# Differential attention and mLSTM block on one core: products of the last attention chunks some steps later, gate products in four groups of 32 output partitions

## The chip, the core and the metric

The kernel runs on one core of a Trainium2 chip. The core has engines that run side by side, each with its own queue of instructions that it works off in order: PE (TensorE, matrix products into the PSUM memory, with its weight loads, PEld), DVE (VectorE), ACT (ScalarE), POOL (GpSimd) and SP (SyncE, which here only issues transfers). Transfers (DMA) run on 16 shared DMA engines. An instruction waits at the head of its queue until what it reads has been written and the buffer that it writes has come free; everything behind it on that engine waits too. The metric is the time of one execution on the device, in microseconds (us); of several runs the median is given.

## The reference, cut to what matters

One layer over x of 1024 rows and 1024 columns. After an RMSNorm one projection gives all inputs of two branches.

```python
xn = _rmsnorm(h, norm_w[layer])
(da_q, da_k, da_v, da_z, ml_q, ml_k, ml_v, ml_o, ml_z, ml_i, ml_f,
 gate_a, gate_m) = [xn @ wp for wp in _split_columns(w_in[layer])]
y_a = _diff_attention(da_q, da_k, da_v, ...) * jax.nn.silu(da_z)
y_m = _mlstm(ml_q, ml_k, ml_v, ml_i, ml_f, ml_o, ...) * jax.nn.silu(ml_z)
merged = g_a * (y_a @ w_pa[layer]) + g_m * (y_m @ w_pm[layer])
h = h + merged @ w_out[layer]
```

The attention branch has 8 heads. For each head and each chunk of 128 queries, two softmaxes over the keys are taken (the keys end with the query's own chunk, so chunk i has (i+1)·128 of them), `attn = probs[0] - lam * probs[1]`, and `attn @ v` is normed over the head's 128 columns (`_rmsnorm(out, subln_w)`). The mLSTM branch has 8 heads as well; its input and forget gates, `ml_i` and `ml_f`, are only 16 of the 11,280 columns of the projection.

## The kernel before, in words

**Numbers as pairs.** Every large product runs in float16 with each operand split into a high and a low part: high·high, high·low and low·high are added in PSUM. So each step of a product is three matmuls: lines 330 to 332 for units with 512 columns, 359 to 361 for units with 256 columns, 856 to 858 for the products with v.

**Phases, units, slots.** The projection is cut into units of 256 weight columns. A phase works off its units on PE and weaves a side program into them. Phase 0 makes q, k, v and z of head 0 (units `aqk` and `avz`). Phases 1 to 7 make those of head h+1 and run `attention(h)`, for heads 0 to 6, as the side program; phase 8 makes gate columns and runs the attention of head 7; then come the mLSTM gates (`if_gates`), the mLSTM heads, and the last projections. A phase with two units has 64 slots, and a plan says at which slot each piece of the side program is issued: an entry (n, name) is due at slot n·8//7, and what is not due by the last slot is issued after it. `PLAN_A` is the plan of heads 0 to 6, `PLAN_C` that of head 7.

**The pieces of attention(h)** (names of the plan, with the chunk's number): `q` makes the scores of the first softmax (line 813 on PE, 823 on DVE, 827 on ACT); `r` makes those of the second, combines both (DVE 838) and turns the result: ACT casts it to float16 (845), DVE takes the low part (846), and SP issues a transposing transfer (848) that lays it down as PE needs it; `v` is the product with v on PE (856 to 858), whose squares ACT sums (859); `f` is the norm's factor for four chunks on POOL (863 to 865); `o` scales four chunks on DVE (871); `t` casts, splits and transposes the result (548 to 550). Chunks 0 to 3 of the product share one bank of PSUM and chunks 4 to 7 another.

**The gate products.** `if_proj` multiplies the 16 gate columns (high and low part side by side, 32 columns, tile `wifp`) with all of x, high and low part, and leaves a table of 32 rows and 1024 columns in device memory (`gif_d`). It runs at the end of phase 0's `aqk` unit, as 2 × 16 matmuls into two PSUM tiles `pmi` of 32 partitions (line 469); ACT copies each out with a scale (472), and SP stores it (473). Much later `if_gates` loads four pieces of it (input and forget gate, each with the high and the low weights, eight heads a piece) and adds them in pairs on DVE (485).

**Buffers around it.** PSUM has three banks `pp` for the units, one pair `psb` for the scores, two `pmi` and one `pvp`. A unit's bank is emptied by ACT and DVE (for `avz` by 568 and 564 on ACT, 569 and 565 on DVE). Tiles of 4 KB per partition come from a ring of 15. The weights of a unit are loaded by SP (226), squared on ACT (245), summed over partitions by a tiny matmul on PE (165), scaled by DVE (135 to 139), and split into parts on ACT (257) and DVE (259).

**What sets the order.** The plan and the weave set the order in which the code asks for instructions. The framework then places them on the engines' queues when the kernel is built, so that an edit can also change the order on an engine at places that it does not name.

Of the kernel before, what the change touches and what calls it, by code (L numbers as in the profile page):

```python
# [10 lines left out]
F32 = mybir.dt.float32  # L11
BF = mybir.dt.bfloat16
I32 = mybir.dt.int32
AF = mybir.ActivationFunctionType
ALU = mybir.AluOpType
AX = mybir.AxisListType

P = 128
S = 1024
D = 1024  # L20
NT = S // P
KC = D // P
H = 8
# [9 lines left out]
OFF_GATE = (9232, 10256)  # L33
BIG = 3.0e38
RING = 15
PLAN_A = [(0, 'q0'), (0, 'r0'), (0, 'q1'), (3, 'r1'), (4, 'q2'), (5, 'r2'), (9, 'q3'), (9, 'r3'), (9, 'q4'), (10, 'v0'), (14, 'v1'), (16, 'r4'), (17, 'q5'), (18, 'v2'), (19, 'r5'), (21, 'q6'), (24, 'r6'), (25, 'q7'), (27, 'r7'), (28, 'v3'), (29, 'v4'), (29, 'v5'), (30, 'f0'), (30, 'o0'), (33, 'v6'), (35, 'v7'), (42, 't0'), (43, 'f1'), (44, 'o1'), (55, 't1')]
PLAN_C = [(0, 'q0'), (0, 'r0'), (6, 'q1'), (7, 'r1'), (7, 'q2'), (9, 'r2'), (16, 'q3'), (19, 'r3'), (19, 'q4'), (19, 'r4'), (19, 'v0'), (22, 'v1'), (22, 'v2'), (25, 'q5'), (28, 'r5'), (29, 'q6'), (31, 'v3'), (32, 'v4'), (33, 'r6'), (37, 'q7'), (38, 'f0'), (38, 'r7'), (46, 'o0'), (52, 'v5'), (52, 'v6'), (63, 'v7'), (64, 'f1'), (67, 'o1'), (82, 't1'), (83, 't0')]
PLAN_M = [(0, '00gate'), (0, '01k0'), (2, '02k1'), (4, '03s0'), (5, '04s1'), (8, '05e0'), (9, '06p0'), (11, '07e1'), (13, '08p1'), (14, '09c0'), (19, '10g00'), (19, '11g01'), (20, '12g02'), (21, '13cp0'), (22, '14bs0'), (22, '15g10'), (25, '16g11'), (25, '17g12'), (26, '18cp1'), (30, '19bs1'), (30, '20g20'), (30, '21g21'), (31, '22cp2'), (32, '23bs2'), (33, '24ch'), (37, '25n0'), (47, '26t0'), (50, '27n1'), (55, '28t1')]
PLAN_N = [(0, '00gate'), (1, '01k0'), (1, '02k1'), (8, '03s0'), (10, '04s1'), (13, '05e0'), (13, '06p0'), (15, '07e1'), (16, '08p1'), (22, '09c0'), (25, '10g00'), (26, '11g01'), (26, '12g02'), (26, '13cp0'), (30, '14bs0'), (31, '15g10'), (36, '16g11'), (37, '17g12'), (40, '18cp1'), (42, '19bs1'), (43, '20g20'), (44, '21g21'), (53, '22cp2'), (54, '23bs2'), (59, '24ch'), (61, '25n0'), (67, '26t0'), (70, '27n1'), (71, '28t1')]
# [9 lines left out]
def block_kernel(ctx, tc, x, norm_w, w_in, lam, subln_w, rel_bias, conv_w, conv_b, b_if,  # L49
                 mh_w, b_gate, w_pa, w_pm, w_out, norm_final, onehot, out):  # L50
    nc = tc.nc
    v, s, g, te = nc.vector, nc.scalar, nc.gpsimd, nc.tensor
# [7 lines left out]
    dram = ctx.enter_context(tc.tile_pool(name="dram", bufs=1, space=bass.MemoryType.DRAM))  # L60
# [15 lines left out]
    def R(dt=F32, shape=None, p="r"):  # L76
        return ring.tile(shape or [P, S], dt, tag="t4", name=nm(p))
# [13 lines left out]
    def s_ps():  # L91
        return psb.tile([P, S], F32, tag="psb", name=nm("psb"))

    def m_ps():
        return pmi.tile([P, 512], F32, tag="pmi", name=nm("pmi"))
# [194 lines left out]
    def x_src(i, th):  # L290
        t = X[th, i // 2]
        return t[:, 0, i % 2, :], t[:, 1, i % 2, :]
# [75 lines left out]
    HS = [slice(0, 512), slice(512, 1024)]  # L368
# [77 lines left out]
    decb = ctile([P, H * NT], p="decb")  # L446
    mcols = ctile([P, 3, NT, H], p="mcols")
    wsc = ctile([P, NT, H], p="wsc")
    gif_d = dram.tile([32, S], F32, tag="gifd", name="gif_d")

    def if_proj():
        ss = sm(cols=2, p="wss")
        s.activation(junk(P), early[:, 384:512], AF.Square, accum_out=ss[:, 0:1])
        v.memset(ss[:, 1:2], 0.0)
        sb, isb = sm(p="sb"), sm(p="isb", bufs=8)
        fnorm_finish(ss, sb, isb)
        sig = sm(p="sig", bufs=8)
        v.tensor_tensor(sig, isb, isx, op=ALU.mult)
        parts = half_tile("wifp").bitcast(F16)[:, :256].rearrange("p (a b) -> p a b", a=KC)
        s.activation(parts[:, :, :16], wif, AF.Copy, scale=sb)  # L460
        v.scalar_tensor_tensor(parts[:, :, 16:], wif, sb, parts[:, :, :16], op0=ALU.mult, op1=ALU.subtract)
        for _ in range(8):
            yield
        t = R(shape=[32, S], p="gif")
        for th in range(2):
            gps = m_ps()
            for i in range(KC):
                for k in range(2):
                    te.matmul(gps[:32, :], parts[:, i, :], x_src(i, th)[k], start=(i + k == 0),
                              stop=(i + k == KC))  # L470
                yield
            s.activation(t[:, HS[th]], gps[:32, :], AF.Copy, scale=sig[:32, :])
        nc.sync.dma_start(gif_d, t)
        yield

    def if_gates():
        gi = R(shape=[H, NT, P], p="gi")
        ff = R(shape=[H, NT, P], p="ff")
        gl = [R(shape=[H, NT, P], p="gl") for _ in range(2)]
        for k, dst in ((0, gi), (1, ff), (2, gl[0]), (3, gl[1])):  # L480
            nc.sync.dma_start(dst.rearrange("h a b -> h (a b)"), gif_d[k * H:k * H + H, :])
        for _ in range(4):
            yield
        for k, dst in ((0, gi), (1, ff)):
            v.scalar_tensor_tensor(dst, dst, bif[:, k:k + 1], gl[k], op0=ALU.add, op1=ALU.add)
        yield
        fl = lambda t: t.rearrange("h a b -> h (a b)")
        af = R(shape=[H, NT, P], p="af")
        v.scalar_tensor_tensor(af, ff, -1.0, ff, op0=ALU.mult, op1=ALU.max)
        s.activation(af, af, AF.Exp, scale=-1.0)  # L490
        s.activation(af, af, AF.Ln, bias=1.0)
        yield
        lf = ff
        v.scalar_tensor_tensor(lf, ff, 0.0, af, op0=ALU.min, op1=ALU.subtract)
        yield
        m = R(shape=[H, NT, P], p="m")
        v.tensor_tensor_scan(fl(m), fl(lf), fl(gi), 0.0, op0=ALU.add, op1=ALU.max)
        yield
        b = af
        for c in range(NT):  # L500
            v.tensor_tensor_scan(b[:, c, :], ones[:H, :], lf[:, c, :], 0.0, op0=ALU.mult, op1=ALU.add)
        yield
        ng = R(shape=[H, NT, P], p="ng")
        v.tensor_tensor(ng, b, m, op=ALU.subtract)
        a = gi
        v.tensor_tensor(a, gi, b, op=ALU.subtract)
        yield
        mprev = ctile([H, NT], p="mprev")
        v.memset(mprev[:, 0:1], 0.0)
        v.tensor_copy(mprev[:, 1:NT], m[:, 0:NT - 1, P - 1])  # L510
        ngl = ctile([H, NT], p="ngl")
        v.tensor_copy(ngl, ng[:, :, P - 1])
        wi = lf
        v.tensor_tensor(wi, ng, mprev.unsqueeze(2).to_broadcast([H, NT, P]), op=ALU.add)
        s.activation(wi, wi, AF.Exp)
        yield
        ws = af
        v.tensor_tensor(ws, a, ngl.unsqueeze(2).to_broadcast([H, NT, P]), op=ALU.add)
        s.activation(ws, ws, AF.Exp)
        yield  # L520
        en = m
        s.activation(en, m, AF.Exp, scale=-1.0)
        dec = ctile([H, NT], p="dec")
        v.tensor_tensor(dec, ngl, mprev, op=ALU.add)
        s.activation(dec, dec, AF.Exp)
        s.dma_start(rows_d[0], fl(ng))
        s.dma_start(rows_d[1], fl(wi))
        s.dma_start(dec_d[0:1, :].rearrange("o (h c) -> (o h) c", c=NT), dec)
        s.dma_start(decb, dec_d[0:1, :].to_broadcast([P, H * NT]))
        yield  # L530
        cps = m_ps()
        for k, t in enumerate((a, ws, en)):
            for c in range(NT):
                o = (k * NT + c) * H
                te.transpose(cps[:, o:o + H], t[:, c, :], ident[:H, :H])
        v.tensor_copy(mcols.rearrange("p a b c -> p (a b c)"), cps[:, :3 * NT * H])
        v.tensor_scalar(wsc, mcols[:, 1], 0.25 * KSC, None, op0=ALU.mult)
        yield
# [529 lines left out]
    for units, side, steps in phases:  # L1068
# [6 lines left out]
        for u in units:  # L1075
# [6 lines left out]
            dst, post = consumers[u.kind](u.idx, u.w)  # L1082
# [62 lines left out]
    for ch in range(4):  # L1145
        w, so = wo[ch].w, [None, None]
        c = slice(ch * 256, ch * 256 + 256)
# [75 lines left out]
```

## Time and profile before

| | |
|---|---|
| median of 3 runs | 1428.03 us (1427.54 to 1428.84) |
| the profiled execution | 1430.35 us |
| its span, first to last instruction | 1428.5 us |
| around the span | 1.85 us |
| mean granted PE clock in the span | 0.994 |

| engine | busy us | share of span |
|---|---|---|
| PE | 1379.5 | 97% |
| PEld | 914.8 | 64% |
| DVE | 849.0 | 59% |
| ACT | 734.3 | 51% |
| POOL | 157.7 | 11% |

Times within the span count from its first instruction. A row of the timeline gives the start, the duration, the engine, the line of the kernel, the operation, the tiles out<-in and a count, and in brackets how long the engine had been idle before it and what ended that. Matmuls overlap, so the distance between two starts, not the duration in the row, is what one matmul costs in a stream. An issue of a transfer stands as SPq (issued by SP) or ACTq (issued by ACT); the transfer lands later. The granted clock is the share of TensorE's full clock that the chip allowed.

### The profile page before, as it was taken

How to read it: one execution, taken by the hardware profiler on the slowest of the kernel's cores; microseconds unless marked ns; L12 is line 12 of the kernel's file. 1: busy time of each engine (PE TensorE's matmuls, PEld its weight loads, DVE VectorE, ACT ScalarE, POOL GpSimd, SP SyncE). 2: the span in 40 equal slices, each digit the busy share in tenths (PEclk: the TensorE clock that was granted, in tenths of full speed). 3: DMA queues.
4: the chain of work that ended last, by engine and by line, in shares of the span. 5: the costliest groups of instructions: out<-in, count | busy, mean ns of one | idle time of the engine just before them, and what ended most of it. 6: DMA issues, size and time to landing. Idle time of an engine off the chain costs nothing.

```text
span 1428.5 us, 25046 instructions
## 1 busy us (share of the span) xinstructions
PE 1379.5 (97%) x9650; PEld 914.8 (64%) x9650; DVE 849.0 (59%) x2310; ACT 734.3 (51%) x1533; POOL 157.7 (11%) x215
## 2 busy tenths in 40 slices
PE   5989999999999999999999999999999999999997
PEld 3657575675756754444586687778769675444786
DVE  6267869678696766433436674765866564233633
ACT  7266657566575667732343444443435344644542
POOL 2001010010100001100102010120211200122004
PEclk9999999999999999999999999999999999999999
DMA  6457366473563634544221413221232135434303
GB/s 200 66 131 154 84 109 136 99 141 84 112 135 87 144 87 117 170 157 129 79 75 60 103 41 94 45 89 45 77 86 75 60 90 158 166 106 164 114 16 118
DMA packets 232585, 150.14 MB, mean 105 GB/s; under 512 B 117297, under 2 KB 209730, under 8 KB 232466
## 3 DMA queue, kind: packets, MB, share of 16 engines
q1 hardware_dynamic: 218450, 123.28, 35.1%
q10 hardware_dynamic: 14016, 25.27, 5.2%
q8 instruction: 75, 1.23, 0.4%
q14 instruction: 44, 0.36, 0.1%
HBM read 90.12 MB, written 18.55 MB: 76 GB/s over the span
## 4 chain that ended last, share of the span: by engine, by line
PE 77%; DVE 8%; DMA 5%; ACT 4%; POOL 3%; issue 2%; SPq 0%; POOLq 0%; DVEq 0%; ACTq 0%
PE pp L330 14%; PE pp L332 14%; PE pp L331 14%; PE pp L359 9%; PE pp L360 9%; PE pp L361 9%; PE psb L813 4%; DMA z<-z 3%; DVE z L823 2%; DMA qw<-rows_d 2%; ACT z L827 1%; DVE wp L259 1%; PE psb L909 1%; DVE z L838 1%; ACT z L845 1%
## 5 line engine op out<-in xcount | busy, mean ns | idle before, releaser
L359 PE MATMUL pp<-wp,X 128*128 128x256 f16 x1280 | 350.4, 274 | 0.0
L360 PE MATMUL pp<-wp,X 128*128 128x256 f16 x1280 | 350.3, 274 | 0.0
L361 PE MATMUL pp<-wp,X 128*128 128x256 f16 x1280 | 350.2, 274 | 0.0
L332 PE MATMUL pp<-X,wp 128*128 128x512 f16 x768 | 291.0, 379 | 1.0 <-DVE wp L259 1.0
L330 PE MATMUL pp<-X,wp 128*128 128x512 f16 x768 | 291.5, 380 | 0.3 <-ACT wp L257 0.3
L331 PE MATMUL pp<-X,wp 128*128 128x512 f16 x768 | 291.3, 379 | 0.0
L257 ACT ACTIVATE wp<-wt,sb 128x512 f16<-128x512 f32 x208 | 137.8, 712 | 110.9 <-DVE sb L138 76.2
L332 PEld LDWEIGHTS <-wp 128*128 128x128 f16 x1024 | 100.0, 98 | 119.3 <-DVE wp L259 1.5
L245 ACT ACTIVATE junk<-wt 128x1024 bf16<-128x1024 f32 x112 | 118.1, 1054 | 100.4 <-DMA wt<-in_w_in_dram 88.0
L330 PEld LDWEIGHTS <-wp 128*128 128x128 f16 x1024 | 100.2, 98 | 102.0 <-issue 1.7
L331 PEld LDWEIGHTS <-wp 128*128 128x128 f16 x1024 | 100.1, 98 | 97.2
L259 DVE SCALAR_TENSOR_TENSOR wp<-wt,sb,wp 128x512 f16<-128x512 f32 x208 | 149.9, 760 | 13.9 <-ACT wp L257 12.2
L359 PEld LDWEIGHTS <-X 128*128 128x128 f16 x1280 | 125.8, 98 | 16.5 <-issue 0.4
L360 PEld LDWEIGHTS <-X 128*128 128x128 f16 x1280 | 125.7, 98 | 16.2
L361 PEld LDWEIGHTS <-X 128*128 128x128 f16 x1280 | 125.7, 98 | 15.7
L827 ACT ACTIVATE z<-z,mx 128x256 f32<-128x256 f32 (+7 forms) x128 | 98.7, 771 | 47.5 <-DVE mx L826 27.1
L823 DVE CUSTOM_DVE_ANT_0 z<-psb,BB,negc 128x256 f32<-128x256 f32 (+7 forms) x128 | 104.1, 813 | 14.9 <-PE psb L813 14.8
L332 PE MATMUL pp<-Y,wp 128*128 128x512 f16 x256 | 97.0, 379 | 0.0
L331 PE MATMUL pp<-Y,wp 128*128 128x512 f16 x256 | 97.0, 379 | 0.0
L330 PE MATMUL pp<-Y,wp 128*128 128x512 f16 x256 | 97.0, 379 | 0.0
L650 DVE SCALAR_TENSOR_TENSOR acc<-up,wcol,acc 128x512 f32<-128x512 f32 x96 | 78.0, 828 | 27.0 <-POOL acc L651 24.8
L813 PE MATMUL psb<-K,Q 128*128 128x512 f16 (+3 forms) x384 | 83.3, 325 | 8.8 <-DMA K<-hl 4.5
(251 smaller groups left out, 2015.8 us busy)
## 6 DMA issues: line engine op xcount, KB each, us to landing
wt<-in_w_in_dram SPq DMA_DIRECT2D x128, 256.0 KB
wt<-in_w_in_dram SPq DMA_DIRECT2D x24, 512.0 KB
K<-hl SPq DMA_DIRECT2D x32, 256.0 KB
gate_d<-tg ACTq DMA_DIRECT2D x32, 256.0 KB
xt<-in_x_dram SPq DMA_DIRECT2D x8, 512.0 KB
Q<-hl SPq DMA_DIRECT2D x32, 128.0 KB
wt<-in_w_pa_dram SPq DMA_DIRECT2D x8, 512.0 KB
ft<-gate_d ACTq DMA_DIRECT2D x16, 256.0 KB
```

The lines of the kernel that those rows point to most:

```text
L245: s.activation(j, w.wt[k], AF.Square, accum_out=ss[:, k:k + 1])
L257: s.activation(dst[0], src, AF.Copy, scale=w.sb)
L259: v.scalar_tensor_tensor(dst[1], src, w.sb, dst[0], op0=ALU.mult, op1=ALU.subtract)
L330: te.matmul(ps, wh, xh, start=(start and i == 0), stop=False, **kw)
L331: te.matmul(ps, wh, xl, start=False, stop=False, **kw)
L332: te.matmul(ps, wl, xh, start=False, stop=(stop and i == n - 1), **kw)
L359: te.matmul(ps[:, o], xh[:, t], wh, start=i == 0, stop=False)
L360: te.matmul(ps[:, o], xh[:, t], wl, start=False, stop=False)
L361: te.matmul(ps[:, o], xl[:, t], wh, start=False, stop=i == KC - 1)
L813: te.matmul(sp[:, c:e], Q[:, p, i * P:(i + 1) * P], K[p][:, j, c:e], start=(j == 0), stop=(j == 1))
L823: v.tensor_tensor_reduce(z[:, :n], sp[:, :n], bb[:, S - n:], negc, BIG, op0=ALU.add, op1=ALU.min, accum_out=mx)
L827: s.activation(z[:, :n], z[:, :n], AF.Exp, bias=mx, scale=-1.0, accum_out=rr[:, 2 * i + p:2 * i + p + 1])
```

## The change

Three things change.

1. `PLAN_A`, for heads 0 to 6: the products with v of chunks 5, 6 and 7 are due later (29, 33, 35 become 30, 35, 40), and so are the factor, the scaling and the output step of the second half (43, 44, 55 become 47, 48, 58). The factor and scaling of the first half now stand ahead of `v5` in the list.
2. The gate products go into four groups of 32 output partitions of one PSUM tile `psb`: one group for each pair of half of x's rows and high or low part. The 32 matmuls keep their size; they are issued round the four groups, and each group sums over its own eight steps. One ACT instruction over 128 partitions copies all out, and ACT's queue, not SP's, stores it.
3. `if_gates` loads six pieces instead of four, each from two places, and adds two more sums on DVE; the products with the high and with the low part of x, which PE added before, are added there (low weights with low x are left out). The ring hands out two more tiles.

```diff
-PLAN_A = [(0, 'q0'), (0, 'r0'), (0, 'q1'), (3, 'r1'), (4, 'q2'), (5, 'r2'), (9, 'q3'), (9, 'r3'), (9, 'q4'), (10, 'v0'), (14, 'v1'), (16, 'r4'), (17, 'q5'), (18, 'v2'), (19, 'r5'), (21, 'q6'), (24, 'r6'), (25, 'q7'), (27, 'r7'), (28, 'v3'), (29, 'v4'), (29, 'v5'), (30, 'f0'), (30, 'o0'), (33, 'v6'), (35, 'v7'), (42, 't0'), (43, 'f1'), (44, 'o1'), (55, 't1')]
+PLAN_A = [(0, 'q0'), (0, 'r0'), (0, 'q1'), (3, 'r1'), (4, 'q2'), (5, 'r2'), (9, 'q3'), (9, 'r3'), (9, 'q4'), (10, 'v0'), (14, 'v1'), (16, 'r4'), (17, 'q5'), (18, 'v2'), (19, 'r5'), (21, 'q6'), (24, 'r6'), (25, 'q7'), (27, 'r7'), (28, 'v3'), (29, 'v4'), (30, 'f0'), (30, 'o0'), (30, 'v5'), (35, 'v6'), (40, 'v7'), (42, 't0'), (47, 'f1'), (48, 'o1'), (58, 't1')]
...
-    gif_d = dram.tile([32, S], F32, tag="gifd", name="gif_d")
+    gif_d = dram.tile([P, 512], F32, tag="gifd", name="gif_d")
...
-        t = R(shape=[32, S], p="gif")
-        for th in range(2):
-            gps = m_ps()
-            for i in range(KC):
+        t = R(shape=[P, 512], p="gif")
+        gps = s_ps()[:, :512]
+        for i in range(KC):
+            for th in range(2):
                 for k in range(2):
-                    te.matmul(gps[:32, :], parts[:, i, :], x_src(i, th)[k], start=(i + k == 0),
-                              stop=(i + k == KC))
-                yield
-            s.activation(t[:, HS[th]], gps[:32, :], AF.Copy, scale=sig[:32, :])
-        nc.sync.dma_start(gif_d, t)
+                    o = (th * 2 + k) * 32
+                    te.matmul(gps[o:o + 32, :], parts[:, i, :], x_src(i, th)[k], start=(i == 0), stop=(i == KC - 1))
+        yield
+        s.activation(t, gps, AF.Copy, scale=sig)
+        s.dma_start(gif_d, t)
         yield
...
-        gl = [R(shape=[H, NT, P], p="gl") for _ in range(2)]
-        for k, dst in ((0, gi), (1, ff), (2, gl[0]), (3, gl[1])):
-            nc.sync.dma_start(dst.rearrange("h a b -> h (a b)"), gif_d[k * H:k * H + H, :])
+        gl = [R(shape=[H, NT, P], p="gl") for _ in range(4)]
+
+        for k, dst in ((0, gi), (1, ff), (2, gl[0]), (3, gl[1]), (4, gl[2]), (5, gl[3])):
+            r = k * H if k < 4 else 32 + (k - 4) * H
+            nc.sync.dma_start(dst.rearrange("h (t a) b -> h t (a b)", t=2),
+                              gif_d.rearrange("(t r) c -> r t c", t=2)[r:r + H])
...
             v.scalar_tensor_tensor(dst, dst, bif[:, k:k + 1], gl[k], op0=ALU.add, op1=ALU.add)
+            v.tensor_tensor(dst, dst, gl[2 + k], op=ALU.add)
```

What stands on the engines' queues differs at three places. From the second half of the gate functions on, the changed kernel's line numbers are higher by 5 (856 becomes 861).

PE, head 0, where the product of chunk 7 with v begins (line 856; `z255` holds its transposed probabilities). The rows ahead are of the `avz` unit of head 1; the tiles X57, X72, X82 and X86 hold its contraction steps in this order, six matmuls to a tile. Before:

```order
L360 MATMUL pp278_1441<-wp231_1107,X86_306 128x256
L361 LDWEIGHTS X86_306
L361 MATMUL pp278_1441<-wp231_1107,X86_306 128x256
L856 LDWEIGHTS z255_1248
L856 MATMUL pmi268_1323<-vr153_644,z255_1248 128x128
```

And now:

```order
L360 MATMUL pp276_1416<-wp226_1083,X72_256 128x256
L361 LDWEIGHTS X72_256
L361 MATMUL pp276_1416<-wp226_1083,X72_256 128x256
L861 LDWEIGHTS z254_1246
L861 MATMUL pmi267_1321<-vr152_642,z254_1246 128x128
```

Two tiles of the unit, 12 matmuls, now stand ahead of it. In numbers of unit matmuls between the products of chunks 4, 5, 6 and 7: 5, 19 and 36 before, 6, 36 and 30 now, and 123 before, 111 now, between chunk 7 and the next head's first scores. The same holds for heads 0 to 6; the tiny matmul 165 keeps its place among the unit's.

ACT, head 0, around the cast of chunk 7 (line 845, now 850, the row with 128x1024 and two z tiles). The rows 859 (now 864) are the squares of chunks 3, 4, 5 and 6, and 245 squares the two halves of a later unit's weights. Before:

```order
L859 ACTIVATE junk_1339,ssq_922<-pmi_1323,rc_921 128x128
L859 ACTIVATE junk_1359,ssq_922<-pmi_1323,rc_921 128x128
L245 ACTIVATE junk_1371,wss_1370<-wt_958 128x1024
L845 ACTIVATE z_1264<-z_1248 128x1024
L245 ACTIVATE junk_1388,wss_1370<-wt_1124 128x1024
L548 ACTIVATE y_1550<-on_1377 128x512
L859 ACTIVATE junk_1423,ssq_922<-pmi_1323,rc_921 128x128
```

And now:

```order
L864 ACTIVATE junk_1337,ssq_920<-pmi_1321,rc_919 128x128
L245 ACTIVATE junk_1349,wss_1348<-wt_956 128x1024
L864 ACTIVATE junk_1378,ssq_920<-pmi_1321,rc_919 128x128
L245 ACTIVATE junk_1386,wss_1348<-wt_1122 128x1024
L850 ACTIVATE z_1262<-z_1246 128x1024
L553 ACTIVATE y_1548<-on_1355 128x512
L573 ACTIVATE vr_1288<-pp_1294 128x256
```

One square of weights moves ahead of chunk 5's, the other ahead of the cast.

ACT, at the end of phase 0, from the square of the second weights on (245). Before:

```order
L245 ACTIVATE junk159_681,wss157_672<-wt143_532 128x1024
L472 ACTIVATE gif147_600<-pmi148_601,sig125_443 32x512
L472 ACTIVATE gif147_600<-pmi149_619,sig125_443 32x512
L568 ACTIVATE vr153_644<-pp155_650 128x256
L257 ACTIVATE wp166_741<-wt128_458,sb161_724 128x512
L257 ACTIVATE wp167_756<-wt128_458,sb161_724 128x512
L564 ACT_TABLE_LOAD
L564 ACTIVATE tz152_643<-pp155_650,hs151_640 128x256
```

And now:

```order
L245 ACTIVATE junk158_679,wss156_670<-wt143_532 128x1024
L257 ACTIVATE wp165_739<-wt128_458,sb160_722 128x512
L257 ACTIVATE wp166_754<-wt128_458,sb160_722 128x512
L257 ACTIVATE wp167_769<-wt143_532,sb160_722 128x512
L257 ACTIVATE wp169_789<-wt143_532,sb160_722 128x512
L473 ACTIVATE gif147_600<-psb148_601,sig125_443 128x512
L573 ACTIVATE vr152_642<-pp154_648 128x256
L474 DMA gif_d_149<-gif147_600 128x512
L569 ACT_TABLE_LOAD
L569 ACTIVATE tz151_641<-pp154_648,hs150_638 128x256
```

All four weight parts now stand ahead of the copy of the gate products, and that copy empties `psb`, which the first scores of head 0 then write. On PE the first scores' second half (`r0`, two matmuls) has moved behind the 51 unit matmuls that followed it.

## The prediction

> **What bounds the kernel now.** I read the page's first part: which engine is busy.
>
> ```profile
> PE 1379.5 (97%) x9650; PEld 914.8 (64%) x9650; DVE 849.0 (59%) x2310; ACT 734.3 (51%) x1533; POOL 157.7 (11%) x215
> ```
>
> PE sets the end: the change is worth what it takes from PE's idle time or from PE's stream, and costs what it adds there. So next I read whom PE waited for, from the list of waits (engine, waiting line, releaser: us in total, times, longest).
>
> ```profile
> PE pmi L856 <- DMA z<-z: 10.7, 8, 2.9
> PE psb L813 <- DMA K<-hl: 4.5, 2, 2.6
> PE pmi L856 <- DVE BB L801: 1.3, 5, 0.3
> PE pmi L856 <- ACT junk L859: 0.8, 5, 0.2
> ```
>
> The products with v (856) lose 12.8 us: to the transposing transfer, and by 2.1 us to small waits at the start of chunks 5 and 6. The timeline of PE tells where the long ones are, one in each of heads 0 to 6 (the bracket is the idle time).
>
> ```profile
> 131.02 0.23 PE L856 MATMUL pmi<-vr,z 128*128 128x128 f16 x1 [0.84 <-DMA z<-z]
> 190.94 0.23 PE L856 MATMUL pmi<-vr,z 128*128 128x128 f16 x1 [1.97 <-DMA z<-z]
> 250.15 0.23 PE L856 MATMUL pmi<-vr,z 128*128 128x128 f16 x1 [1.35 <-DMA z<-z]
> 309.37 0.23 PE L856 MATMUL pmi<-vr,z 128*128 128x128 f16 x1 [1.74 <-DMA z<-z]
> 368.11 0.23 PE L856 MATMUL pmi<-vr,z 128*128 128x128 f16 x1 [0.81 <-DMA z<-z]
> 428.87 0.23 PE L856 MATMUL pmi<-vr,z 128*128 128x128 f16 x1 [2.87 <-DMA z<-z]
> 489.32 0.23 PE L856 MATMUL pmi<-vr,z 128*128 128x128 f16 x1 [0.88 <-DMA z<-z]
> ```
>
> All seven are the first matmul of chunk 7: its 24 matmuls follow. PE gets there before the turned probabilities have landed.
>
> **The plan: work moved ahead of the wait.** PE now does 12 more matmuls of the `avz` unit before chunk 7 (the rows above: X86 before, X72 of the next pass now). What one costs is read at the end of phase 0, where 144 of the same kind run without a gap; first and last row:
>
> ```profile
> 57.96 0.28 PE L359 MATMUL pp<-wp,X 128*128 128x256 f16 x1
> 73.58 0.27 PE L361 MATMUL pp<-wp,X 128*128 128x256 f16 x1
> ```
>
> (73.58 − 57.96) / 143 = 0.109 us from start to start, so 12 × 0.109 = 1.31 us of work goes ahead of each wait. A head can gain this much and no more, and no more than its idle time. Beside the waits of the rows stand 2.1 / 7 = 0.30 us a head in chunks 5 and 6 (one more unit matmul stands ahead of chunk 5, 17 more ahead of chunk 6, so these go too). Idle time by head: 1.14, 2.27, 1.65, 2.04, 1.11, 3.17, 1.18. Each cut at 1.31, the sum is **8.67 us**.
>
> This holds if the transfer lands when it did. What issues it, in head 0:
>
> ```profile
> 122.67 0.37 ACT L859 ACTIVATE junk<-pmi,rc 128x128 bf16<-128x128 f32 x1 [1.31 <-PE pmi L858]
> 123.16 1.06 ACT L245 ACTIVATE junk<-wt 128x1024 bf16<-128x1024 f32 x1
> 124.22 1.06 ACT L845 ACTIVATE z<-z 128x1024 f16<-128x1024 f32 x1
> 125.18 1.04 ACT L245 ACTIVATE junk<-wt 128x1024 bf16<-128x1024 f32 x1
> 125.30 1.23 DVE L846 TENSOR_TENSOR z<-z,z 128x1024 f16<-128x1024 f32 x1 [0.40 <-ACT z L845]
> 126.56 4.42 DMA z<-z
> ```
>
> The cast (845) at 124.22 releases DVE's low part, this the transfer at 126.56 (this last row is of the chain, where the transfer's piece lasts until it landed, 130.98), and PE starts at 131.02. Two squares of weights (245) now stand ahead of the cast instead of one. The first moves into the 1.31 us in which ACT waited for chunk 5: it takes 1.06 us (123.16 to 124.22) and fits. The second takes the place that the first had, and the cast starts when it did, or later by the one unit matmul that now stands ahead of chunk 5, 0.1 us. This costs nothing where a head's idle time is used up, and 0.1 us in the four heads where some is left (1, 2, 3, 5): **+0.4 us**. Bounds of the cast's delay: 0 (ACT's gap holds both), and 1.1 us (the first square does not fit, a whole square later). I take 0.1, by the 1.31 us gap.
>
> **The clock in head 5.** Windows of equal length after chunk 7's start in heads 5 and 0 (after the window's length: PE, PEld, DVE, ACT, POOL busy with counts, granted clock, DMA share, GB/s):
>
> ```profile
> 428.87:432.74 3.87, 3.87 (x33) 3.39 (x33) 0.51 (x1) 1.30 (x3) 0.69 (x2) 0.56 0.98 244
> 131.02:134.89 3.87, 3.87 (x48) 3.61 (x49) 2.54 (x4) 3.00 (x7) 1.92 (x3) 1.00 0.92 199
> ```
>
> After the wait of 2.87 us the granted clock was 0.56 and 15 matmuls fewer were done: 15 × 0.109 = 1.6 us. No other head shows it, so a wait near 2 us did not bring it on, and head 5 will be left with 3.17 − 1.31 = 1.9. Another execution need not have it; bounds are 0 and 1.6, I count half, **−0.8 us**, because one head of seven is too little to say how often it comes. The Trainium skill (page "TensorE: Matmul & The Clock Gate", section "What's actually happening") has PE fall to half clock after at least one idle window of about 3.4 us. The trace had it after 2.87 us, and the measurement decides; by the page's figure this term would be zero and the sum 0.8 us smaller.
>
> **The front: five microseconds of products, and who waits there.** The 32 gate products start at 50.95 and the unit behind them at 57.96: 7.01 us. What follows, on PE, ACT, DVE and SP:
>
> ```profile
> 50.95 7.08 PE L469 MATMUL pmi<-X,wifp 128*32 128x512 f16 x32
> 74.33 0.16 PE L165 MATMUL pmi<-s,ones 128*128 128x1 bf16 x1 [0.47 <-ACT gif L472]
> 77.05 0.27 PE L813 MATMUL psb<-K,Q 128*128 128x128 f16 x2 [2.56 <-DMA K<-hl]
> 79.29 0.37 PE L813 MATMUL psb<-K,Q 128*128 128x128 f16 x2 [1.96 <-DMA K<-hl]
> 79.45 0.42 PE L359 MATMUL pp<-wp,X 128*128 128x256 f16 x1
> 72.56 1.06 ACT L245 ACTIVATE junk<-wt 128x1024 bf16<-128x1024 f32 x1 [20.90 <-DMA wt<-in_w_in_dram]
> 73.61 1.23 ACT L472 ACTIVATE gif<-pmi,sig 32x512 f32<-32x512 f32 x2
> 74.75 0.36 ACT L568 ACTIVATE vr<-pp 128x256 f16<-128x256 f32 x1
> 75.14 1.33 ACT L257 ACTIVATE wp<-wt,sb 128x512 f16<-128x512 f32 x2
> 76.49 1.28 ACT L564 ACT_TABLE_LOAD   x1
> 77.79 0.47 ACT L564 ACTIVATE tz<-pp,hs 128x256 f32<-128x256 f32 x1
> 78.29 0.42 DVE L565 SCALAR_TENSOR_TENSOR tz<-tz,pp 128x256 f32<-128x256 f32 x1 [0.32 <-ACT tz L564]
> 69.32 0.35 SPq L585 DMA_DIRECT2D strip<-tb_d  x1
> ```
>
> The bill for PE is made here by transfers. ACT waits 20.90 us for weights that land at 72.5; SP issues `strip`, and behind it Q and K, only from 69.32; neither hears of PE. PE fills its three banks until 73.85 and then waits for ACT and for K. If the four groups run side by side, PE merely arrives some 5 us earlier at the same wait; if they run one behind the other, it arrives as before. Both give **0**. The Trainium skill (same page, section "Measured speedup vs the span model") has three column groups of 512 columns run 2.38 times as fast; an estimate by it is 7.01 / 2.38 = 2.9 us, a gain of 4.1, and no trace here shows it yet.
>
> What moves is the end of this wait, through ACT's new order. The tiny matmul 165 no longer waits for the copy (0.47 us sooner at most; I take 0.3), so the four parts (257, 1.33 / 2 = 0.64 apart) run from about 74.8 to 77.35. Then come the copy (1.23 / 2 = 0.62, to 77.95), `vr` (0.36), the table load (1.28, to 79.5), `tz` (0.47) and DVE's 0.42, which empties the first bank at 80.4. PE's first scores, which now need `psb` from the copy, start at 78.0, not 77.05; unit matmuls resume at 80.45, not 79.45: **+1.0 us**. Bounds: +0.5, if the half clock ends when it did so that the lost stretch is a slow one (the row at 79.45 runs 0.42, the one at 73.58 0.27); +2.7, by head 0's first turn, whose scores are now behind 51 matmuls:
>
> ```profile
> 83.70 14.14 SPq L848 DMA_TRANSPOSE z<-z  x3
> L856 PE MATMUL pvp<-vr,z x80: 219/219/219, 96.6 to 534.3; 128*128 128x128 f16 x80
> ```
>
> The turn's transfer was issued 4.4 us after those scores (79.29 to 83.70). They now come at about 88.9 (80.45, 24 matmuls at 0.21, 24 at 0.11, three at 0.22), so the transfer is issued at 93.3 and lands at 97.7 if it takes 4.42 us; chunk 0's product is due at 96.6 + 1.0. With a landing 1.6 us slower it waits 1.7.
>
> **The gates later.** Two loads and two sums more, the sums by the nearest row; the row behind it (of the chain) is where PE first reads the gates, in 24 small transposes.
>
> ```profile
> 558.76 1.27 DVE L485 SCALAR_TENSOR_TENSOR ff<-ff,bif,gl 8x1024 f32<-8x1024 f32 x1
> 646.67 1.58 PE pmi L535 x24
> ```
>
> 2 × 1.27 = 2.5 us on DVE, 88 us ahead of PE's first use. The cover is PE's own stream of gate and output units in between, in which the list of waits has no entry for the gates. I count **0**; without the cover 2.5. The loads stand on SP ahead of chunk 7's transfer of head 7 and wait for transfers alone.
>
> **Sum:** −8.67 + 0.4 − 0.8 + 0 + 1.0 + 0 = −8.1 us. The profiled execution took 1430.35 (span 1428.5 and 1.85 around it), 2.3 above the median of 1428.03; the terms are differences, so I take them from the median: 1428.03 − 8.1 = **1419.9 us**. Ends of this case: −8.67 − 1.6 + 0.5 = −9.8, or 1418.2; and with a cast 0.5 us late in all seven heads, no clock term and the dear front, −8.67 + 3.5 + 2.7 = −2.5, or 1425.5.
>
> **The rivals.**
>
> *The landing moves along.* If the first square does not fit into ACT's gap, the cast and the transfer come 1.06 us later, and of 1.31 us moved only 0.25 a head is left: −1.75 + 1.0 = −0.7, or 1427.3. For it: both squares do stand ahead of the cast, and the spare time is 1.31 − 1.06 = 0.25 us. Against: ACT's wait there ended with PE's chunk 5, which hardly moves. Chance 0.13.
>
> *The gate products' time reaches the end.* If four groups run as one, 7.01 × 3/4 = 5.3 us more go: 1414.6. It needs transfers that land with PE. Against it: 69.32 and 72.56 are set by transfers. The Trainium skill's rule on column groups, named above, speaks for the speed, not for the place. Chance 0.04.
>
> *Slower: the cast waits for weights.* The second square now runs at about 123.2 ahead of the cast, and its weights were needed only at 125.18. If they land as late as that, the cast comes 2.05 us later, which the 1.31 us no longer cover: 0.74 × 7 = 5.2, with the front +6.2, or 1434.2. It decides from a delay of 1.31 us on. Against it: the weights' issue,
>
> ```profile
> 105.45 1.08 SPq L226 DMA_DIRECT2D wt<-in_w_in_dram  x2
> ```
>
> 18 us ahead of that square. Chance 0.05.
>
> **How the numbers follow.** Forecast 0.78, rivals 0.13, 0.04 and 0.05. About 0.2% (2.9 us) is what a measurement of this kernel tells from no change. Faster by more: the forecast but for its upper tail, and the second rival, 0.79; within: 0.15; slower: the third rival and a front dearer than its bound, 0.06. The range holds the forecast's ends and reaches up to the first rival, and down by one more drop of the clock (3.87 us at half speed, 1.9) that the runs may have had elsewhere: 1416.3 to 1427.5. The forecast's own is 1418.2 to 1425.5.
>
> **What would show it.** In the changed trace the first matmul of chunk 7 waits for nothing in heads 0, 4 and 6, and about 0.4, 0.8, 1.1 and 2.0 us in heads 2, 3, 1 and 5; the cast of chunk 7 starts at the same distance from chunk 7's scores, within 0.2 us. The gate products end well before 57.96, PE then idles some 5 us longer at 165, and unit matmuls resume near 80.4. From 560 us on no new wait of PE appears. The prediction is wrong if chunk 7's transfer is issued a microsecond later, if PE resumes at the front several us later, or if a wait opens behind chunk 7 because ACT and DVE empty banks later there.

## The result, and the profile after

| | before | changed |
|---|---|---|
| median | 1428.14 us (4 runs, 1427.54 to 1428.84) | 1416.83 us (4 runs, 1415.80 to 1417.01) |
| profiled execution, its span | 1430.35, 1428.5 us | 1417.01, 1415.2 us |

The ratio is 0.9919, with a 95% interval of 0.9902 to 0.9936. The kernel became 11.3 us faster where 8.1 were forecast: the right side and inside the range, 0.5 us from its lower end, and beyond the forecast's own end of 1418.2.

In the rows of the changed kernel the lines from 491 on have moved by five (856 is 861, 845 is 850, 813 is 818) and the gate products' line 469 is 471. Its page, first part, as before:

```profile
PE 1372.3 (97%) x9650; PEld 912.0 (64%) x9650; DVE 848.1 (60%) x2312; ACT 734.3 (52%) x1532; POOL 157.1 (11%) x215
```

The list of PE's waits (us in total, times, longest) of the changed kernel:

```profile
PE pmi L165 <- DVE s L159: 4.0, 1, 4.0
PE psb L818 <- ACT gif L473: 3.8, 1, 3.8
PE pmi L861 <- DMA z<-z: 2.5, 3, 1.1
PE pp L359 <- DVE tz L570: 2.3, 1, 2.3
```

The wait for the turned probabilities fell from 10.7 us in eight places to 2.5 in three, and the small waits ahead of chunks 5 and 6 (2.1 us) are gone from the list. Against that stand 10.1 us of waits at the front, where before there were 5.0. The timeline shows which three heads still wait ahead of chunk 7:

```profile
189.39 0.23 PE L861 MATMUL pmi<-vr,z 128*128 128x128 f16 x1 [1.10 <-DMA z<-z]
304.58 0.23 PE L861 MATMUL pmi<-vr,z 128*128 128x128 f16 x1 [0.33 <-DMA z<-z]
420.48 0.23 PE L861 MATMUL pmi<-vr,z 128*128 128x128 f16 x1 [1.05 <-DMA z<-z]
```

They are heads 1, 3 and 5; in the other four PE waits 0.10 us or less there.

**Where the time went, by place.** The unit matmuls are the same 7680 in the same order in every kernel here, so the distance between the same two of them in two traces tells what a stretch gained. From the 289th on, each 288 of them are one head:

| head | 0 | 1 | 2 | 3 | 4 | 5 | 6 | sum |
|---|---|---|---|---|---|---|---|---|
| before, us | 58.32 | 59.92 | 59.21 | 59.22 | 58.73 | 62.41 | 58.80 | 416.61 |
| changed, us | 57.11 | 58.48 | 57.48 | 57.71 | 57.47 | 58.43 | 57.52 | 404.20 |

The seven heads gave 12.4 us of the 13.3 by which the two spans differ. The front gave nothing. First the line groups of the first unit matmuls (330) and of the early chunks' products with v (861), of the changed kernel, with their first and last starts:

```profile
L330 PE MATMUL pp<-X,wp x768: 376/379/634, 17.0 to 1236.6; 128*128 128x512 f16 x192
L861 PE MATMUL pvp<-vr,z x80: 219/219/219, 96.5 to 521.7; 128*128 128x128 f16 x80
```

Before, these were 17.4 and 96.6 (to 534.3): the changed execution began its matmuls some 0.5 us earlier and came out of the front 0.1 us earlier, so the front cost it 0.4 us in this pair of traces. At the end of the early chunks it is 12.6 us ahead, and behind them only fractions of a microsecond shift (13.1 ahead at the last unit matmul). The profiled execution of before was 2.2 us above its median, so 13.3 in the spans and 11.3 in the medians agree.

### The profile page after: what moved, and what is told of

It is laid out like the page before. It is cut to its first block, busy times and chain, and to the rows that moved or that the text cites. A ratio compares the mean times of both kernels' runs of the same rounds, so it can differ in the third digit from the quotient of the medians.

```text
span 1415.2 us, 25057 instructions
## 1 busy us (share of the span) xinstructions
PE 1372.3 (97%) x9650; PEld 912.0 (64%) x9650; DVE 848.1 (60%) x2312; ACT 734.3 (52%) x1532; POOL 157.1 (11%) x215
## 4 chain that ended last, share of the span: by engine, by line
PE 78%; DVE 8%; DMA 5%; ACT 5%; issue 2%; POOL 2%; SPq 0%; POOLq 0%; DVEq 0%; ACTq 0%
PE pp L330 14%; PE pp L332 14%; PE pp L331 14%; PE pp L359 8%; PE pp L360 8%; PE pp L361 8%; PE psb L818 4%; DMA z<-z 2%; DMA wt<-in_w_in_dram 2%; DVE z L828 2%; ACT z L832 1%; DMA qw<-rows_d 1%; DVE z L851 1%; PE psb L914 1%; DVE wp L259 1%
```

## The experiments

### The plan alone, and the gates alone

The first kernel is the kernel before with the new table `PLAN_A`, the second the changed kernel with the old one.

```diff
-PLAN_A = [..., (29, 'v4'), (29, 'v5'), (30, 'f0'), (30, 'o0'), (33, 'v6'), (35, 'v7'), ...]
+PLAN_A = [..., (29, 'v4'), (30, 'f0'), (30, 'o0'), (30, 'v5'), (35, 'v6'), (40, 'v7'), ...]
```

> Only the plan's new table; the gate products as before. Theory (the plan is the whole gain): PE's waits ahead of the products with v fall from 12.8 us to about 2.5 us as in the changed kernel, so the median falls by 10 to 11.5 us, to 1417 to 1418; the front (unit matmuls resume near 79.4 us) stays as before. Rival (the gate products give part of it): a fall of 6 to 8 us only, to 1420 to 1422, and the rest turns up when the gates alone are changed.

> Only the gate products in four groups, their table and the later sums; the plan as before. Theory (the front is set by transfers): the 32 products take about 1.8 us instead of 7.0 us and PE then waits some 5 us longer; the median stays within 0.8 us of before, 1427.3 to 1428.9, and the waits ahead of chunk 7 stay at 10 to 13 us. Rival (the gate products' time reaches the end): 4 to 5 us less, 1423 to 1424.

The plan alone took 1417.2 us, a ratio of 0.9915 (0.9901 to 0.9928). The gates alone took 1428.66 us, a ratio of 1.000 (0.9991 to 1.0008). PE's waits with the plan alone:

```profile
PE psb L813 <- DMA K<-hl: 4.7, 2, 2.5
PE pmi L856 <- DMA z<-z: 3.2, 5, 1.2
```

and with the gates alone:

```profile
PE pmi L861 <- DMA z<-z: 9.9, 8, 2.8
PE pmi L165 <- DVE s L159: 4.0, 1, 4.0
```

The plan is the whole gain, and the gate products in four groups change the time by less than can be measured: each part moves its own wait and leaves the other's.

### How much work ahead of the wait pays: half, and three times as much

```diff
-(35, 'v6'), (40, 'v7'), (42, 't0')
+(35, 'v6'), (39, 'v7'), (42, 't0')     six unit matmuls earlier than in the changed kernel
+(35, 'v6'), (42, 't0'), (43, 'v7')     24 later
```

> The changed kernel with chunk 7's products six unit matmuls earlier, so that half of the work that was moved ahead of its wait (12 x 0.109 = 1.31 us a head) is taken back. Theory (the landing is fixed, moved work pays one to one): each head loses 6 x 0.109 = 0.65 us, so 4.6 us in seven heads, and the median is near 1421.4. Rival (the landing follows the order of ACT and SP): another amount, or none.

> The changed kernel with chunk 7's products put behind 24 more unit matmuls (24 x 0.109 = 2.6 us more work ahead of each wait). Theory (work put ahead of a fixed landing pays until the idle time is used up): the 2.5 us that were left of the waits in heads 1, 3 and 5 go and nothing else changes, about 2.5 us under the changed kernel, near 1414.3. Rival (the landing or the next stage moves along): the same time as the changed kernel or more, 1416.8 or above, with a new wait of PE behind chunk 7 (a bank that is emptied later, or the next head's scores).

> The late plan with grouped gates once more, on one chip side by side with the spare products, since the two were timed on different chips (1412.25 and 1412.4 us). Both theories: 1412 to 1412.6, half clock from about 71 to 84.5 us in its profile.

| six earlier, changed, 24 later: us per head | 0 | 1 | 2 | 3 | 4 | 5 | 6 | sum |
|---|---|---|---|---|---|---|---|---|
| six earlier | 57.82 | 59.03 | 58.12 | 58.33 | 58.09 | 59.09 | 58.26 | 408.74 |
| changed | 57.11 | 58.48 | 57.48 | 57.71 | 57.47 | 58.43 | 57.52 | 404.20 |
| 24 later | 56.90 | 57.21 | 57.20 | 57.21 | 57.20 | 57.20 | 57.26 | 400.18 |

Six earlier: 1421.3 us (ratio 0.995, 0.9935 to 0.9965), and 4.54 us more over the seven heads, where 6 × 0.109 × 7 = 4.6 were expected. Its wait, by the list:

```profile
PE pmi L861 <- DMA z<-z: 7.4, 7, 1.7
```

24 later: 1412.25 us (0.9881, 0.9866 to 0.9896), and once more 1413.24 us (0.9889, 0.9875 to 0.9904). The wait for the turned probabilities is no longer in its list, no other took its place, and heads 1 to 6 take 57.2 us each, head 0 56.9. Head 1's first matmul of chunk 7 now has no idle time before it:

```profile
190.28 0.27 PE L361 MATMUL pp<-wp,X 128*128 128x256 f16 x1
190.38 0.22 PE L861 MATMUL pmi<-vr,z 128*128 128x128 f16 x1
```

So the landing does not follow the products: from the last scores to the start of chunk 7 a head takes the same, within 0.11 us, in the changed kernel and with six earlier. Work moved ahead of the landing pays one to one until nothing is left to wait for; the change stopped short of that. This version beats both kernels.

It gained more than the 2.5 us expected: 4.0 in the heads. In head 4 of the changed kernel PE waits 0.09 us ahead of chunk 7, yet the head takes 0.27 us more than with no wait. A wait costs its idle time and some 0.2 us besides: idle time counts from the end of the matmul before, whose row runs 0.27 us, while in a stream the next one starts 0.1 us after its start, as in the rows above.

### The gate products, one group after the other

```diff
-        for i in range(KC):
-            for th in range(2):
-                for k in range(2):
+        for th in range(2):
+            for k in range(2):
+                for i in range(KC):
```

> The changed kernel with the same 32 gate products in another order: all eight of one group of 32 output partitions, then the next group, instead of the four groups in turn. All other orders are unchanged. Theory: products of neighbouring groups overlap and those of one group do not, so the 32 take 7.0 us again (32 x 0.219) instead of 1.84 us, and the time stays that of the changed kernel within 0.6 us, near 1416.8, since PE only arrives later at the same wait. Rival one: the speed has nothing to do with the order, the products take 1.84 us again. Rival two: the products' time reaches the end, 4 to 5 us more, near 1421.5.

The timeline of PE in the changed kernel (first) and in this one:

```profile
50.48 1.91 PE L471 MATMUL psb<-X,wifp 128*32 128x512 f16 x32
52.32 0.28 PE L359 MATMUL pp<-wp,X 128*128 128x256 f16 x1
```

```profile
51.18 4.54 PE L471 MATMUL psb<-X,wifp 128*32 128x512 f16 x32
55.65 0.28 PE L359 MATMUL pp<-wp,X 128*128 128x256 f16 x1
```

In turn the 32 products take 1.84 us (before 7.01, so 3.8 times as fast): their starts stand 0.003 to 0.004 us apart in fours, and 0.21 between the fours. One group after the other they take 4.47 us, not 7.0: at each change of group several products of the old and the new group still start in pairs. So the speed comes from the order, as expected, but the loss in the other order was over-estimated. The time did not follow: 1417.52 us, ratio 0.9919 (0.9906 to 0.9933), against 0.9919 for the changed kernel. PE came 2.6 us later to the same place and waited that much less there (1.4 us instead of 4.0):

```profile
PE psb L818 <- ACT gif L473: 3.8, 1, 3.8
PE pp L359 <- DVE tz L570: 2.3, 1, 2.3
PE pmi L165 <- DVE s L159: 1.4, 1, 1.4
```

### The transfer that the front waits for, taken away

The table of all heads goes to device memory in one transfer early. Here head 0's part goes alone, and the rest behind head 0's Q and K. Both kernels have chunk 7's products 24 later; the second has the old gate products. The diff is cut to the two transfers.

```diff
-        nc.sync.dma_start(tb_d.rearrange(...)[:, :, :384], tb.unsqueeze(1).to_broadcast([H, P, 384]))
+        nc.sync.dma_start(tb0_d.rearrange(...)[:, :, :384], tb[0:1, :].unsqueeze(1).to_broadcast([1, P, 384]))
...
         s.dma_start(gif_d, t)
+        nc.sync.dma_start(tb_d.rearrange(...)[:, :, :384], tb[1:H, :].unsqueeze(1).to_broadcast([H - 1, P, 384]))
```

> The kernel with the late plan (chunk 7's products 24 unit matmuls later than in the changed kernel, 1412.25 us) and the grouped gate products, in which the bias table of head 0 alone is written to device memory early and that of heads 1 to 7 only behind head 0's Q and K. This takes away the transfer that the front is thought to wait for (in the changed kernel the first strip of the table is loaded at 68.85 us and the weights land at 70.6). Theory (the front is set by transfers): the weights, the strip and K land before PE has done its 144 unit matmuls at about 68 us, the 10 us of waits there (4.0, 3.8 and 2.3 us) go, and the time falls by 8 to 10 us to 1402 to 1404. Rival (something else sets the front, ACT's chain or the order): it stays within 2 us of 1412. Second rival: the rest of the table, 30 us of transfer, now holds up the next weights, and a wait of PE after 85 us gives most of it back.

> The same late plan and the same split of the table, with the gate products in their old form (two passes of 16, 7.0 us) and the old sums. Theory: with the transfers out of the way PE's own work sets the front, so the 5.2 us between 7.0 and 1.84 us are heard now: about 5 us above the kernel with grouped products beside it. Rival (the products' time never reaches the end, whatever the transfers do): the same time as that kernel within 1 us.

The front with grouped products, ACT and PE:

```profile
51.13 1.05 ACT L245 ACTIVATE junk<-wt 128x1024 bf16<-128x1024 f32 x1
68.90 2.56 ACT L257 ACTIVATE wp<-wt,sb 128x512 f16<-128x512 f32 x4 [16.63 <-DVE sb L138]
74.72 0.40 PE L359 MATMUL pp<-wp,X 128*128 128x256 f16 x1 [2.37 <-DVE tz L573]
```

The weights are there at 51 us instead of 70.7, and unit matmuls resume at 74.72 instead of 78.72 with the table in one piece. With the old products beside it:

```profile
57.57 0.28 PE L359 MATMUL pp<-wp,X 128*128 128x256 f16 x1
77.74 0.39 PE L359 MATMUL pp<-wp,X 128*128 128x256 f16 x1 [0.76 <-DVE tz L568]
```

Now the products are heard, though by less than the 5 us expected: the resume differs by 3.0 us, the end of head 6, counted from the first unit matmul, by 1.3, and the medians by 2.0 (1419.39 and 1421.35 us; ratios 0.9938, 0.9921 to 0.9954, and 0.9952, 0.9938 to 0.9967; the intervals overlap). So the transfers did hide at least a part of them. But the first theory had the front wrong in size: the resume came only 4 us earlier, not 10. With the weights landed, ACT still waits 16.63 us, now for the tiny matmul 165, which stands behind all 144 unit matmuls on PE, and ACT's copies and the table load stand behind that. And the second rival came true as well. The rest of the table held up the next weights, whose issue took 32 us, and PE waited for what is made of later ones:

```profile
56.34 32.36 SPq L226 DMA_DIRECT2D wt<-in_w_in_dram  x4
112.50 0.16 PE L165 MATMUL pmi<-s,ones 128*128 128x1 bf16 x1 [2.93 <-DVE s L159]
114.04 0.27 PE L359 MATMUL pp<-wp,X 128*128 128x256 f16 x1 [1.38 <-ACT wp L257]
```

Head 0 took 67.47 us, 10.6 more than with the table in one piece. These waits are 4.3 of it, one step at half clock from 114.49 to 117.90 us adds to it, and the order on PE, which the edit also changed, may hold the rest. As a version it is worse than what it started from.

### The half clock at the front

Twelve spare products that feed nothing are put on PE: `warm` issues three of them behind each of the four high weight parts of one unit, for which alone `busy` is true (its definition is left out here).

```diff
             s.activation(dst[0], src, AF.Copy, scale=w.sb)
+            if busy:
+                warm(3, dst[0][:, 0, :P], dst[0])
```

> The kernel with the late plan and grouped gates (1412.25 us), its table as it was, with twelve spare products of 512 columns on PE behind the tiny matmul at 72.2 us, three behind each of the four weight parts, into a bank that is not in use yet; their result is not read. They do no work for the output. Theory (in the profiles PE resumes at 78.8 us and runs at half clock to 84.6, some 6 us in which it does half the work): the spare products run from 73.6 to 78.7 us at half clock, the full clock comes one or two of its 3.41 us steps earlier, at 77.7 or 81.1, and the time falls by 1.7 to 3 us, to about 1410. Rival (the clock comes when it came, or the later scores of head 0 cost as much): 1412 to 1415.

> The same with the twelve spare products. In their profile the full clock came at 77.3 instead of 84.5 us and the unit matmuls were 2.0 us further at 87 us, yet the medians were equal. Theory (the clock is worth what the profile shows): about 1.5 us under the kernel beside it. Rival (other executions have the clock's steps elsewhere, or the later scores cost as much): within 0.6 us of it.

Windows of the same 6 us (length, then PE, PEld, DVE, ACT, POOL busy with counts, granted clock, DMA share, GB/s), first without and then with the spare products, both from the second pair:

```profile
78.50:84.50 6.00, 5.10 (x25) 3.61 (x26) 1.87 (x5) 3.20 (x9) 0.00 (x0) 0.50 1.04 297
```

```profile
78.50:84.50 6.00, 4.97 (x42) 3.88 (x41) 2.35 (x8) 3.31 (x9) 0.00 (x0) 1.00 1.06 263
```

The clock did come some 7 us earlier, and PE did 42 instead of 25 matmuls. The time did not fall: 1412.4 and 1412.72 us against 1412.25 and 1413.24 without (ratios 0.9889, 0.9875 to 0.9904, and 0.9882, 0.9866 to 0.9899). The rival holds, within 0.6 us. In the second pair the resume came 1.3 us later with the spare products, but 1.0 of that is weights that landed later in that execution (first without, then with; line 255 is 245 there):

```profile
71.22 1.06 ACT L245 ACTIVATE junk<-wt 128x1024 bf16<-128x1024 f32 x1 [19.48 <-DMA wt<-in_w_in_dram]
72.20 1.06 ACT L255 ACTIVATE junk<-wt 128x1024 bf16<-128x1024 f32 x1 [20.66 <-DMA wt<-in_w_in_dram]
```

Head 0 took 57.82 instead of 56.90 us, of which 0.76 is one wait for its later scores. So their place took back a part of what the clock gave, not all: at the 351st unit matmul, counted from the first, the kernel with spare products is still 0.5 us ahead in the second pair and 1.4 in the first. Behind head 6, where these kernels have the same plan, their four profiles scatter by 1.6 us, so that the medians can neither show nor exclude a gain of this size.

### Another profile of the kernel before

> The kernel before, unchanged, for another profile of it. Theory (a wait of nearly 3 us ahead of chunk 7 in head 5 brings the clock down): head 5's transfer takes about 1 us longer than in heads 0, 4 and 6 again, PE waits 2.7 to 2.9 us there, and the granted clock is 0.5 for one step of 3.41 us behind it. Rival (the drop was chance): no step of half clock behind the wait.

```profile
428.53 0.23 PE L856 MATMUL pmi<-vr,z 128*128 128x128 f16 x1 [2.93 <-DMA z<-z]
428.52:432.39 3.87, 3.86 (x32) 3.43 (x33) 0.47 (x1) 1.30 (x3) 0.69 (x2) 0.56 1.00 248
```

The wait in head 5 is 2.93 us and the clock behind it 0.56 again. The profile with the gates alone shows the same (2.76 us, 0.56). All three profiles with the old plan have it, and none of the ten with chunk 7's products moved has it in head 5. The changed kernel's window after chunk 7's start:

```profile
420.48:424.35 3.87, 3.87 (x48) 3.61 (x49) 0.66 (x2) 1.88 (x5) 1.49 (x3) 1.00 0.96 223
```

The drop was no chance of one execution. In these three profiles the wait starts 0.1 to 0.4 us behind the start of a step of the clock (the steps are described at the end).

## Why the prediction was right, and where its sizes were off

| step of the prediction | forecast, us | measured in the two traces, us |
|---|---|---|
| work ahead of the wait, heads 0 to 6 | −8.67 | −10.8 |
| the cast later | +0.4 | 0.0 |
| half clock in head 5 | −0.8 | −1.65 |
| gate products in four groups | 0 | 0 (alone: ratio 1.000) |
| the front's wait ends elsewhere | +1.0 | +0.4 |
| gates later | 0 | 0 |

The measured terms come to −12.05 us; with the 0.5 us by which the changed execution began earlier and 0.5 us behind 870 us, where no step of the change lies, they make up the 13.1 us at the last unit matmul. That the median lies inside the range is in part luck: the 1.9 us below the forecast's own end were kept for one more drop of the clock elsewhere, which did not come; the 1.4 us that the median lies beyond that end are the first term's, above all transfers that landed sooner.

**Work moved ahead of the wait.** The mechanism was right: the step from 6 to 12 unit matmuls pays one to one (4.54 us, 4.6 by count), and with 36 no wait is left. The term was undersized by 2.1 us. In head 5 the transfer landed 1.0 us sooner after its issue than before, in heads 2 and 3 0.4 and 0.2: 1.65 us that the step "if the transfer lands when it did" held at zero. The other 0.45 are 0.07 to 0.15 us in each of heads 0, 1, 4 and 6: in the timeline the small waits ahead of chunks 5 and 6 come to 0.37 us a head, not the 0.30 that the list's 2.1 us gave, and the wait's own 0.2 us ahead of chunk 6 went with the wait.

**The cast.** It did not move: 

```profile
122.58 0.37 ACT L864 ACTIVATE junk<-pmi,rc 128x128 bf16<-128x128 f32 x1
123.07 1.06 ACT L245 ACTIVATE junk<-wt 128x1024 bf16<-128x1024 f32 x1
124.13 1.06 ACT L850 ACTIVATE z<-z 128x1024 f16<-128x1024 f32 x1
```

The first square fitted into ACT's gap, the second took the place the first had had, and the cast starts at 124.13 instead of 124.22, as much earlier as head 0 itself began. It starts 6.59 or 6.60 us after the last scores in every one of these heads, in both traces. With it fall the rival in which the landing moves along and the slower one in which the cast waits for weights: neither has a trace here.

**The clock.** Counted half because one head of seven showed it; it was there in all three profiles with the old plan, so the whole 1.65 us counted. The step that failed is the halving. But counted from the program's first instruction the clock's steps start up to 1.75 us apart in the thirteen profiles, so an execution in which the wait falls otherwise is not excluded.

**The gate products and the front.** Zero was right, and the reason holds as far as it went: ACT waits for weights, in order, whatever PE does. The end of the wait was mis-sized, because the step took 72.56 us for the weights' landing as given:

```profile
70.61 1.06 ACT L245 ACTIVATE junk<-wt 128x1024 bf16<-128x1024 f32 x1 [19.42 <-DMA wt<-in_w_in_dram]
73.01 2.56 ACT L257 ACTIVATE wp<-wt,sb 128x512 f16<-128x512 f32 x4 [1.25 <-DVE sb L138]
75.47 0.67 ACT L473 ACTIVATE gif<-psb,sig 128x512 f32<-128x512 f32 x1
78.83 0.40 PE L359 MATMUL pp<-wp,X 128*128 128x256 f16 x1 [2.27 <-DVE tz L570]
```

They landed at 70.6, the chain behind them ran as worked out (copy, `vr`, table load, `tz`, one bank), and PE resumed at 78.83, not 80.45. That early resume then ran at half clock until 84.7, so the front as a whole still lost 0.4 us. So little cannot be told from none: two profiles of the kernel with 24 later differ by 0.3 us over the same stretch, and the gates alone took 0.7 less than before. The sooner landing does not come from the gate products, so it was luck: ACT's idle time before it was 19.43 us with the plan alone, which has the old products, 20.91 in the second profile of before, and 20.66 once with grouped products (19.42 in the changed kernel). Why it varies, no run here settles.

**What was stated as a test.** Heads 0, 4 and 6 were to wait for nothing and wait less than 0.1 us; heads 2, 3, 1 and 5 were to wait 0.4, 0.8, 1.1 and 2.0 us and waited 0.10, 0.33, 1.10 and 1.05. PE idles 5.1 us longer at the front, as said. No new wait of PE appeared behind 560 us, and the two sums more on DVE are not heard.

## What to carry to other kernels

Where PE waits for a transfer that is issued a fixed time after PE's own earlier work, put independent matmuls ahead of the wait until none is left, with some to spare: each pays its own length and the last one ends the wait's restart too. A faster stretch of PE is worth nothing ahead of a wait for transfers; take the transfer away before pricing it, and then look at what stands in order behind it on every engine. A wait that leaves one step of the clock nearly idle costs a step at half clock as well; here it did in every profile of the old plan, so count such a loss in full.

## What the runs showed of the hardware

**A transposing transfer is slow beside an instruction packet.** Why do heads 1, 3 and 5 wait longest, with any plan? The view of transfers for 5.5 us around the chunk 7 transfer (the GB/s in 40 slices, then the queues), before, head 5 (421.9 to 427.4) and head 4 (363.1 to 368.6):

```profile
GB/s 209 238 89 238 119 119 328 357 268 328 179 119 151 136 335 171 138 43 52 43 73 54 52 17 19 21 7 9 19 114 285 283 292 289 289 292 290 290 289 565
q8 instruction: 1, 0.02, 1.3%
q14 instruction: 1, 0.01, 0.4%
```

```profile
GB/s 119 298 119 179 238 60 298 328 447 387 268 119 37 99 201 214 205 205 214 225 223 218 227 209 218 216 209 220 192 194 233 438 155 30 268 179 179 238 89 268
```

In head 5 the flow falls to 7 to 73 GB/s for more than 1.5 us, from 424.2 us on; an instruction packet of 16,384 bytes is on its way from 423.9 to 425.0. Packets of 256 bytes that start beside it take up to 1.96 us, where the longest in head 4's window takes 0.23.

In the profiles before, before again, gates alone, plan alone, changed, serial and six earlier an instruction packet of queue 8 starts between the issue and chunk 7's start in heads 1, 3 and 5 and in none of the others. From issue to chunk 7's start pass 5.37 to 5.77 us in head 1, 4.67 to 4.97 in head 3 and 5.49 to 6.53 in head 5, against 4.44 to 4.73 in heads 0, 4 and 6 (once 4.80) and 4.51 to 4.58 in head 2 (4.70 with the plan alone, once 4.96). That the packet is the cause was not tried with a run of its own, but the kernels with spare products come close: there the packet starts 0.9 to 1.8 us ahead of the issue in heads 1 and 3, and once in head 5, and by the traces' landing records these five transfers landed 4.26 to 4.64 us after issue, against 4.76 to 5.65 for the same heads with the same plan and no spare products. The Trainium skill (page "Runtime: NRT & Kernel Launch", section "Instruction fetch mechanics") has engines fetch code in blocks of 16 KiB through a DMA queue, at a cost that is mostly hidden. The size agrees with this packet; if it is the cause, its cost was not hidden for the transfer beside it.

In head 5 a second packet, the one of queue 14 in the view, goes with the longest waits: under the old plan it starts 4.9 to 5.0 us after the issue, and the last of the transfer's 16 landing records comes 0.8 to 0.9 us behind the other 15; under the new plans it starts 1.2 to 1.4 us after the issue, and no record stands apart. (In head 0 of both profiles with 24 later it starts 3.9 us after the issue, and the last record is 0.6 us behind.) That would be most of the 1.0 us by which head 5 was sooner; it was not tried either.

**The clock goes in fixed steps of 3.41 us, and one nearly idle step is enough.** Windows cut at these steps, before, head 5:

```profile
425.83:429.24 3.41, 0.54 (x9) 0.37 (x8) 3.39 (x10) 2.40 (x4) 1.08 (x2) 1.00 1.08 213
429.24:432.65 3.41, 3.41 (x29) 2.94 (x27) 0.14 (x1) 1.21 (x3) 0.60 (x2) 0.50 1.01 253
```

and the changed kernel's front:

```profile
77.91:81.33 3.42, 2.50 (x12) 1.80 (x13) 1.87 (x5) 2.07 (x7) 0.00 (x0) 0.50 1.06 320
81.33:84.74 3.41, 3.41 (x18) 2.43 (x16) 0.00 (x0) 1.59 (x3) 0.00 (x1) 0.50 0.88 244
```

In each trace all changes of the clock lie on one grid of 3.413 us: in the trace of before at 77.66, 84.49, 429.24 and 432.65, which are 0, 2, 103 and 104 steps from the first. A step with 0.54 us of work was followed by one at half clock; one with 2.50 us of work at half clock was not followed by full clock, one with 3.41 was.

Over all steps of the thirteen traces, from the first record of the clock (19 to 26 us) on, those at full clock with up to 1.32 us of busy PE were followed by half clock and those with 1.54 or more never; at half clock, 2.60 us or less was never followed by full clock and 2.84 or more always. The Trainium skill (page "TensorE: Matmul & The Clock Gate", section "What's actually happening") has the same free-running window of 3.41 us and asks for one idle window; here 2.87 us of idleness sufficed because they filled most of one step.
